# A hybrid decoder layer on one core: a new stage order, whole first transfers and a longer warm-up

## The chip, the cores and the metric

The kernel runs on one core of a Trainium2 chip. The metric is the device time of one execution in microseconds; the median of three runs is given. An execution was also recorded by the hardware profiler, and all rows of the trace come from it.

A core has five engines with instruction streams of their own: TensorE (PE in the rows; its weight loads, PEld, overlap its matmuls), VectorE (DVE), ScalarE (ACT), GpSimd (POOL) and SyncE (SP), which here issues all transfers between HBM and the on-chip memories. Engines wait for each other through semaphores.

## The reference

One layer of a decoder serves a prompt of 1024 tokens and a group of 8 sequences with 8 new tokens each (64 rows). With `D_MODEL = 1024`, the width is cut into attention A (384), convolution B (384) and memory attention M (256):

```python
hp = rmsnorm(x, norm_pre)
qa, ka, va, ga, ab, bb, gb, qm, gm = split(hp @ w_in)     # 25 blocks of 128 columns
oa = dilated_mix(rope(qa), rows, rope(ka), va)   # windows (128,1),(512,4),(2048,16), causal, 6 heads
u  = ab * sigmoid(bb)                            # GLU
ob = conformer_tail(depthwise_causal(u, w_dw))   # 31 taps, LayerNorm, swish, w_pw2
mk, mv = rmsnorm(mem_prompt) @ w_mem_kv          # 256 memory tokens, 4 heads
om = mem_attend(qm, mk, mv)
y  = x + rmsnorm(concat(oa * silu(ga), ob * silu(gb), om * silu(gm)) @ w_out, norm_post)
```

The sample group does the same with its caches: 2048 cached keys and values for A, a convolution state for B, and cached memory keys and values for M. Outputs are `y` for both groups, the new keys, values and convolution states, and both window caches shifted by the 8 new rows, which is a copy from HBM to HBM of some 50 MB in 32 transfers.

## The kernel before

**One recorded program.** The kernel does not call the engines as it goes. A class `Plan` records every operation with the buffers that it reads and writes; `schedule` then simulates the five engines with a cost model of its own, and from this comes, while the kernel is built, one fixed order of instructions for each engine. `issue` (L441, the line of nearly all rows of the trace) emits them in that order. On an engine, the ready operation of the lowest `level` goes first, and among those the one recorded first. So a place in the program is a priority, and a waiting operation is overtaken by later ones that are ready. Ten is the ordinary level; the convolution's taps are at 20, as filler on VectorE, and the 32 cache copies at 60, issued only when the modelled DMA is free. On the chip the order is fixed: an instruction that waits holds up everything behind it on its engine.

**Where the order comes from.** `ORDER` lists the stages in the order in which they are recorded: `kk`, `qq`, `vv` with a number are the projections of keys, queries and values of head pair 0 to 2, `at` the prompt's attention of that pair, `cb` a block of the convolution (its projections and then its taps), `mp` and `mk` the memory tokens' norm and projection, `kn` the sample group's new keys, `qm` the memory queries, `ma` and `ms` memory attention of the prompt and of the samples, `ga`, `gb` and `gm` gate blocks, `ct` the convolution's tail (LayerNorm and `w_pw2`), `sm` the samples' masks, `sk` and `sv` scores on the sample caches' keys and the sums over their values, `wo` the loading of the output weights, and `ot` output tiles of 128 rows, each with 24 matmuls for each half of its columns.

**Tiles and buffers.** Tokens lie along the free axis: `xT` comes as 8 tiles of 128 features by 1088 tokens. A value of 32 bits is multiplied as a high and a low part (`whi`, `wlo` for weights; pairs of `gen` tiles for x), with three matmuls in place of one. A projection block is 8 x 3 matmuls over token ranges of 512, 256 and 320 columns, 72 in all. Buffers are slots with a tag, taken when an operation that needs one is scheduled, and given back when its last user is done: `raw` (2 slots) for weights as loaded, `whi` and `wlo` (2 each) for their parts, `gen` (33) for most tiles of 128 x 1088, `tab` (2) for tables, `sm` for small columns, `mm`, `S` and `tp` for PSUM banks. A load can thus be issued only when the model sees its slot free. The sample caches come as tiles of 512 KB: `kneA` and `kneB` for keys, `vneA` and `vneB` for values; their sums are many matmuls of 32 output columns (`mm<-gen,pt`).

**The start.** `WARM` matmuls on a zero tile run on TensorE while the first transfers are under way. The first x tile and the first weights are each loaded in two pieces. Each x tile is split by `norm_split`, on ScalarE (high part) and VectorE (low part). RMSNorm's row scales need x a second time with tokens along the partitions: nine `xn` tiles, squared by ScalarE with a running sum (`squares_of`), then turned by transposes on TensorE (`rstd_of`, tile `sm` to `tp`) into a row `rstd` in a `tab` slot, with which queries and keys are scaled.

**Masks and tables.** The prompt's mask is the second `tab` tile. The samples' masks `smA` (128 x 1024) and `smB` (128 x 320) are in `gen` slots. The post-norm weights `gpost` (128 x 1024) take a `tab` slot at `wo`.

Of the kernel before, what the change touches and what calls it, by code (L numbers as in the profile page):

```python
# [21 lines left out]
KB = 8  # L22
SEQ = 1024
NS = 64
T = SEQ + NS
WARM = 12
CH = ((0, 512), (512, 768), (768, 1088))
# [93 lines left out]
class Plan:  # L121
# [148 lines left out]
    def schedule(self):  # L270
# [13 lines left out]
        port = {"V": 0.0, "G": 0.0}  # L284
        events, order, dma_free = [], [], 0.0
        table, setup, pe_end, warm = None, None, -1e9, 0
# [22 lines left out]
        now = 0  # L309
        while events:  # L310
            now = events[0][0]
# [13 lines left out]
            for e, q in queues.items():  # L325
# [4 lines left out]
                while q:  # L330
# [8 lines left out]
                    early = False  # L339
# [36 lines left out]
                if o.calls:  # L376
                    c = on(o, e)
# [6 lines left out]
                cost = o.cost  # L384
# [5 lines left out]
                if e == "PE":  # L390
                    if now - pe_end > self.COLD:
                        warm = now + 4500
                    if now < warm:
                        cost *= 2
                    if o.setup != setup:
                        cost += 95
                    setup = o.setup
                    pe_end = now + cost
# [57 lines left out]
BLOCKS += [("gb", _i) for _i in range(3)] + [("ga", _i) for _i in range(3)] + [("gm", 0), ("gm", 1)]  # L456
ORDER = "kk0 vv1 qq0 cb1 vv0 qq1 at0 kk1 at1 kk2 cb0 vv2 qq2 at2 ga0 mp cb2 qm1 kn mk qm0 ma1 ga1 ma0 ms1 ct sm ga2 gm1 sk0 sk1 gm0 sv0 gb0 gb1 gb2 wo ot2 sk2 ms0 sv1 sv2 ot4 ot0 ot7 ot8 ot1 ot3 ot5 ot6"
NAMES = dict(kk="qk", qq="qk", vv="v", at="attn", cb="conv", ct="convtail", mp="memkv", mk="memkv", kn="knew", ma="memattn",
# [6 lines left out]
def hybrid_kernel(ctx: ExitStack, tc: tile.TileContext, a: dict):  # L465
# [144 lines left out]
    for k in range(KB):  # L610
        x = t_("gen", [128, T])
        hi, lo = (t_("gen", [128, T], F32R, loose=True) for _ in range(2))
        cuts = [slice(0, 512), slice(512, T)] if k == 0 else [slice(0, T)]
        if k == 0:
            w = t_("raw", [128, KB, 128])
            first[BLOCKS[0]] = w
            SP.dma_start(w[:, early[0], :], a["w_in"][INDEX[BLOCKS[0]]][:, early[0], :])
        for c in cuts:
            SP.dma_start(x[:, c], a["xT"][k][:, c])
        if k == 0:  # L620
            SP.dma_start(w[:, early[1], :], a["w_in"][INDEX[BLOCKS[0]]][:, early[1], :])
        if k == 3:
# [666 lines left out]
    for n_, part in enumerate(parts):  # L1289
# [33 lines left out]
        elif kind == "sm":  # L1323
            smA, smB = t_("gen", [128, 1024]), t_("gen", [128, 320])
            SP.dma_start(smA, a["smA"])
# [131 lines left out]
```

## Time and profile before

| | before |
|---|---|
| runs, us | 600.92, 602.62, 603.91 |
| median of the runs, us | 602.62 |
| profiled execution, us | 600.98 |
| its span, first to last instruction, us | 599.2 |
| mean granted clock of TensorE, share of full speed | 0.989 |
| TensorE busy, us | 578.3 (97%) |
| VectorE busy, us | 441.3 (74%) |
| ScalarE busy, us | 298.2 (50%) |
| GpSimd busy, us | 124.1 (21%) |
| moved by DMA, MB | 134.96 |

The span is what the rows of the trace add up to; the execution's own time has a little around it. A clock of 1.00 in a stretch means 2.4 GHz throughout, 0.50 would be 1.2 GHz throughout. In a row of a timeline, the number in brackets is the idle time of the engine ahead of that row, and behind the arrow stands the engine, and the tile, whose work ended it. Names such as `gen` are tags, without the number of the slot.

### The profile page before, as it was taken

How to read it: one execution, taken by the hardware profiler on the slowest of the kernel's cores; microseconds unless marked ns; L12 is line 12 of the kernel's file. 1: busy time of each engine (PE TensorE's matmuls, PEld its weight loads, DVE VectorE, ACT ScalarE, POOL GpSimd, SP SyncE). 2: the span in 40 equal slices, each digit the busy share in tenths (PEclk: the TensorE clock that was granted, in tenths of full speed). 3: DMA queues.
4: the chain of work that ended last, by engine and by line, in shares of the span. 5: the costliest groups of instructions: out<-in, count | busy, mean ns of one | idle time of the engine just before them, and what ended most of it. 6: DMA issues, size and time to landing. Idle time of an engine off the chain costs nothing.

```text
span 599.2 us, 11301 instructions
## 1 busy us (share of the span) xinstructions
PE 578.3 (97%) x4466; PEld 482.5 (81%) x4466; DVE 441.3 (74%) x829; ACT 298.2 (50%) x644; POOL 124.1 (21%) x101
## 2 busy tenths in 40 slices
PE   6999999999999999999899999999999899999995
PEld 3889998778789998789898898887778667777885
DVE  4629999989993999999999999982544744226333
ACT  5676423596751138861667596761525434223221
POOL 0006644132401461011042303540000000000000
PEclk9999999999999999999999999999999799999999
DMA  8997291999996556896656032109869789781321
GB/s 300 321 379 250 76 230 51 356 333 366 309 332 249 162 145 207 332 346 193 230 201 212 34 108 73 36 4 330 310 223 379 286 323 394 284 308 73 93 101 70
DMA packets 38500, 134.96 MB, mean 225 GB/s; under 512 B 11248, under 2 KB 17904, under 8 KB 37424
## 3 DMA queue, kind: packets, MB, share of 16 engines
q1 hardware_dynamic: 38448, 134.25, 64.4%
q8 instruction: 35, 0.57, 0.4%
q14 instruction: 17, 0.14, 0.1%
HBM read 124.31 MB, written 58.87 MB: 306 GB/s over the span
## 4 chain that ended last, share of the span: by engine, by line
PE 71%; DMA 9%; DVE 8%; ACT 8%; SPq 2%; issue 2%; DVEq 0%; ACTq 0%
PE mm L441 59%; PE S L441 8%; DVE gen L441 6%; PE tp L441 5%; ACT gen L441 4%; DMA gen<-in_vneA 3%; DMA gen<-in_xn 2%; DMA gen<-in_xT 2%; SPq L441 2%; ACT e L441 2%; DMA gen<-in_kneB 1%; DMA out_cvs<-uc 1%; ACT whi L441 1%; DVE ck L441 1%; DVE e L441 1%
## 5 line engine op out<-in xcount | busy, mean ns | idle before, releaser
L441 PE MATMUL mm<-gen,whi 128*128 128x512 f32 (+3 forms) x1488 | 382.4, 343 | 4.7 <-ACT gen L441 3.7
L441 PEld LDWEIGHTS mm<-gen,whi 128*128 128x128 f32 (+1 forms) x1488 | 256.0, 189 | 38.9 <-issue 5.2
L441 PE MATMUL mm<-gen,wlo 128*128 128x512 f32 (+2 forms) x728 | 247.2, 340 | 0.0
L441 PEld LDWEIGHTS mm<-gen,wlo 128*128 128x128 f32 x728 | 137.6, 189 | 14.9 <-issue 2.8
L441 DVE SCALAR_TENSOR_TENSOR gen<-gen,cst,gen 128x1024 f32<-128x1024 f32 (+3 forms) x107 | 137.3, 1286 | 3.2 <-ACT gen L441 2.4
L441 ACT ACTIVATE whi<-raw 128x1024 fp32r<-128x1024 f32 (+1 forms) x29 | 30.5, 1052 | 58.4 <-PE mm L441 51.4
L441 ACT ACTIVATE gen<-gen 64x256 fp32r<-64x256 f32 (+6 forms) x87 | 47.2, 549 | 23.2 <-POOL gen L441 11.8
L441 ACT ACT_TABLE_LOAD x34 | 43.6, 1283 | 7.7 <-DVE sm L441 4.0
L441 ACT ACTIVATE e<-e,sm 128x320 f32<-128x320 f32 (+8 forms) x57 | 33.7, 592 | 18.3 <-DVE sm L441 17.9
L441 PE MATMUL S<-gen,gen 128*128 128x256 f32 (+7 forms) x448 | 40.5, 297 | 1.6 <-ACT gen L441 1.4
L441 PE MATMUL tp<-ident,e 128*128 128x128 f32 (+1 forms) x239 | 40.0, 278 | 0.9 <-ACT gen L441 0.5
L441 DVE TENSOR_TENSOR ck<-mm,tab 128x512 f32<-128x512 f32 (+2 forms) x48 | 25.1, 529 | 19.4 <-PE mm L441 17.9
L441 POOL TENSOR_TENSOR wlo<-raw,whi 128x1024 fp32r<-128x1024 f32 x10 | 27.3, 2734 | 57.5 <-ACT whi L441 57.5
L441 POOL TENSOR_TENSOR gen<-gen,ck 128x256 f32<-128x256 f32 (+3 forms) x17 | 16.6, 985 | 107.9 <-ACT ck L441 92.0
L441 POOL TENSOR_TENSOR pr<-uc,cst 128x496 f32<-128x496 f32 x12 | 22.1, 1838 | 72.1 <-DVE gen L441 49.9
L441 DVE TENSOR_TENSOR gen<-gen,gen 64x256 fp32r<-64x256 f32 (+4 forms) x46 | 33.6, 739 | 3.5 <-PE mm L441 1.5
L441 DVE CAST whi<-gen 128x128 fp32r<-128x128 f32 (+1 forms) x23 | 4.5, 224 | 42.7 <-PE mm L441 42.7
L441 ACT ACTIVATE e<-mm 128x512 f32<-128x512 f32 (+2 forms) x20 | 11.4, 572 | 48.6 <-PE mm L441 48.6
L441 PEld LDWEIGHTS S<-gen,gen 64*32 64x32 f32 (+1 forms) x448 | 27.6, 135 | 7.7 <-issue 2.9
L441 PEld LDWEIGHTS tp<-ident,e 128*128 128x128 f32 (+1 forms) x239 | 27.1, 137 | 8.3 <-issue 3.0
L441 DVE TENSOR_TENSOR wlo<-raw,whi 128x1024 fp32r<-128x1024 f32 (+2 forms) x20 | 25.4, 1268 | 3.0 <-ACT whi L441 2.9
L441 ACT ACTIVATE ck<-ck 128x512 f32<-128x512 f32 (+2 forms) x33 | 16.2, 502 | 21.7 <-DVE ck L441 21.6
(127 smaller groups left out, 691.6 us busy)
## 6 DMA issues: line engine op xcount, KB each, us to landing
out_wk_s<-in_kc SPq DMA_DIRECT2D x16, 1530.0 KB
out_wv_s<-in_vc SPq DMA_DIRECT2D x16, 1530.0 KB
raw<-in_w_in SPq DMA_DIRECT2D x24, 512.0 KB
gen<-in_kneA SPq DMA_DIRECT2D x24, 512.0 KB
gen<-in_vneA SPq DMA_DIRECT2D x24, 512.0 KB
gen<-in_xn SPq DMA_DIRECT2D x8, 512.0 KB
raw<-in_w_out SPq DMA_DIRECT2D x8, 512.0 KB
raw<-in_xn SPq DMA_DIRECT2D x8, 512.0 KB
```

What stands on the lines that cost most here:

```text
L441: getattr(o.real, o.method)(*[real(x) for x in o.args], **{k: real(v) for k, v in o.kw.items()})
```

## The change

Six things are edited. `WARM` rises from 12 to 18. The first x tile and the first weights are each loaded in one transfer; the weights' splitting into parts stays in two cuts (`early`). In the planner, the modelled DMA is free from 2000 ns on and not from 0, a matmul after one of another tile shape costs 105 ns and not 95, and one of the same shape behind a gap costs 80 ns more than before. `ORDER` is a new list. And `smB` moves from a `gen` slot to a `tab` slot.

```diff
-WARM = 12
+WARM = 18
...
-        events, order, dma_free = [], [], 0.0
+        events, order, dma_free = [], [], 2000.0
...
                     if o.setup != setup:
-                        cost += 95
+                        cost += 105
+                    elif now > pe_end + 1:
+                        cost += 80
                     setup = o.setup
...
-ORDER = "kk0 vv1 qq0 cb1 vv0 qq1 at0 kk1 at1 kk2 cb0 vv2 qq2 at2 ga0 mp cb2 qm1 kn mk qm0 ma1 ga1 ma0 ms1 ct sm ga2 gm1 sk0 sk1 gm0 sv0 gb0 gb1 gb2 wo ot2 sk2 ms0 sv1 sv2 ot4 ot0 ot7 ot8 ot1 ot3 ot5 ot6"
+ORDER = "kk0 vv0 qq0 vv1 cb1 qq1 at0 kk1 at1 kk2 cb0 vv2 qq2 at2 ga0 mp cb2 kn qm1 ga1 mk qm0 ga2 ma1 ma0 ms1 ct sm sk0 gm1 sk1 gm0 gb1 gb2 sv0 gb0 wo ot1 ot2 ms0 sv1 sk2 ot6 ot0 ot3 ot4 sv2 ot7 ot8 ot5"
...
         cuts = [slice(0, 512), slice(512, T)] if k == 0 else [slice(0, T)]
+        SP.dma_start(x, a["xT"][k])
         if k == 0:
-            w = t_("raw", [128, KB, 128])
-            first[BLOCKS[0]] = w
-            SP.dma_start(w[:, early[0], :], a["w_in"][INDEX[BLOCKS[0]]][:, early[0], :])
-        for c in cuts:
-            SP.dma_start(x[:, c], a["xT"][k][:, c])
-        if k == 0:
-            SP.dma_start(w[:, early[1], :], a["w_in"][INDEX[BLOCKS[0]]][:, early[1], :])
+            first[BLOCKS[0]] = load_w(BLOCKS[0])
...
-            smA, smB = t_("gen", [128, 1024]), t_("gen", [128, 320])
+            smA, smB = t_("gen", [128, 1024]), t_("tab", [128, 320])
```

What the planner makes of it shows in the order of each engine's instructions; three places are shown. The two numbers behind a tag in a name are counts, which shift with the program; the tag ahead of them is what to read. L441 of before is L443 of the changed kernel.

At the start of SyncE's order, its first loads before (`raw` is a weight tile, `gen<-in_xT` an x tile, the last number its width):

```order
L441 DMA raw_7_116<-in_w_in 128x256
L441 DMA gen_9_119<-in_xT 128x512
L441 DMA gen_9_119<-in_xT 128x576
L441 DMA raw_7_116<-in_w_in 128x768
L441 DMA gen_15_126<-in_xT 128x1088
L441 DMA gen_17_129<-in_xT 128x1088
```

And now:

```order
L443 DMA gen_7_116<-in_xT 128x1088
L443 DMA raw_9_119<-in_w_in 128x1024
L443 DMA gen_11_122<-in_xT 128x1088
L443 DMA gen_13_125<-in_xT 128x1088
L443 DMA gen_15_128<-in_xT 128x1088
```

Two issues fewer stand ahead of the second x tile. The third load of `w_in`, which stood ahead of all `xn` tiles, now stands behind the second of them.

On SyncE, the loads of the values of the first sample pair, among loads of output weights, before (a part of the twelve):

```order
L441 DMA gen_4094_5058<-in_vneA 128x1024
L441 DMA gen_4105_5071<-in_vneA 128x1024
L441 DMA gen_4108_5075<-in_vneA 128x1024
L441 DMA raw_4111_5079<-in_w_out 128x1024
L441 DMA gen_4123_5094<-in_vneA 128x1024
L441 DMA gen_4129_5102<-in_vneB 128x1024
L441 DMA gen_4142_5118<-in_vneB 128x1024
L441 DMA gen_4145_5122<-in_vneA 128x1024
L441 DMA raw_4148_5126<-in_w_out 128x1024
L441 DMA gen_4160_5140<-in_vneA 128x1024
L441 DMA gen_4165_5148<-in_vneA 128x1024
L441 DMA gen_4183_5170<-in_vneA 128x1024
```

And now:

```order
L443 DMA gen_4068_5027<-in_vneA 128x1024
L443 DMA raw_4079_5042<-in_w_out 128x1024
L443 DMA gen_4139_5115<-in_vneA 128x1024
L443 DMA raw_4149_5127<-in_w_out 128x1024
L443 DMA gen_4156_5136<-in_vneB 128x1024
L443 DMA gen_4167_5149<-in_vneB 128x1024
L443 DMA raw_4173_5156<-in_w_out 128x1024
L443 DMA gen_4177_5161<-in_vneA 128x1024
L443 DMA gen_4190_5177<-in_vneA 128x1024
L443 DMA raw_4196_5184<-in_w_out 128x1024
L443 DMA gen_4200_5189<-in_vneA 128x1024
L443 DMA gen_4203_5193<-in_vneA 128x1024
```

Two more `vneA` loads stand ahead of the rows shown of now. These first three go into slots that the keys leave; from `gen_4139` to `gen_4203` the burst holds ten transfers.

On TensorE, the memory tokens' projection (`mm` 128x256, its low weights `wlo`), before; the three matmuls on `qs` are the transposes of the new keys and the two on `sm` those of the memory's row scales:

```order
L441 MATMUL mm_2608_3252<-gen_133_292,whi_2451_3077 128x320
L441 MATMUL mm_2608_3252<-gen_124_282,wlo_2465_3094 128x320
L441 MATMUL mm_2642_3289<-ident_166,qs_607 64x128 x3
L441 MATMUL tp_2645_3293<-ident_166,sm_2313_2918 128x128 x2
L441 MATMUL mm_2647_3296<-gen_2350_2962,whi_2543_3177 128x256
L441 MATMUL mm_2647_3296<-gen_2366_2983,whi_2543_3177 128x256
L441 MATMUL mm_2647_3296<-gen_2350_2962,wlo_2559_3196 128x256
```

And now, at the new keys' transposes, and then at the memory's:

```order
L443 MATMUL mm_2549_3184<-ident_149,qs_611 64x128 x3
L443 MATMUL mm_2553_3189<-gen_25_143,whi_2448_3072 128x512
...
L443 MATMUL mm_2728_3385<-gen_136_295,whi_2548_3182 128x320
L443 MATMUL mm_2728_3385<-gen_128_286,wlo_2561_3200 128x320
L443 MATMUL tp_2759_3420<-ident_149,sm_2362_2973 128x128 x2
L443 MATMUL mm_2761_3423<-gen_2404_3023,whi_2656_3305 128x256
L443 MATMUL mm_2761_3423<-gen_2423_3045,whi_2656_3305 128x256
L443 MATMUL mm_2761_3423<-gen_2404_3023,wlo_2678_3330 128x256
```

The 144 matmuls of `qm1` and `ga1` have moved in between the two; `ga2` too now stands ahead of both blocks of the prompt's memory attention, of which one had `ga1` ahead of the other, and `gm1` alone is left to mix with them. In the same way the values of the last pair (`sv2`) have moved behind four output tiles, 106 of whose matmuls stand between the last pair's keys and them, and the first block of the convolution (`cb1`) stands behind one more value projection. Over the whole order TensorE changes tile shape between matmuls 130 times, where it was 138 times.

## Rows read from the trace of the kernel before

**Rows 1.** Section 1 of the page: busy us (share of the span) and instructions.

```profile
PE 578.3 (97%) x4466; PEld 482.5 (81%) x4466; DVE 441.3 (74%) x829; ACT 298.2 (50%) x644; POOL 124.1 (21%) x101
```

**Rows 2.** Stretches: length; busy PE, PEld, DVE, ACT, POOL; granted clock; DMA share; GB/s.

```profile
10.00:20.00 10.00, 8.14 (x36) 7.00 (x37) 9.09 (x8) 8.80 (x8) 0.00 (x0) 0.83 1.02 350
...
290.00:300.00 10.00, 8.05 (x63) 7.43 (x62) 9.30 (x18) 7.14 (x14) 0.00 (x0) 1.00 0.44 141
...
460.00:470.00 10.00, 6.94 (x131) 5.10 (x133) 8.31 (x24) 6.82 (x21) 0.94 (x3) 0.84 0.98 383
...
sum 599.20, PE 578.33 PEld 482.54 DVE 441.29 ACT 298.24 POOL 124.07; mean PE 9.64 PEld 8.04 DVE 7.35 ACT 4.97 POOL 2.07
```

**Rows 3.** TensorE in order of time: begin, us, what, [idle before, what ended it].

```profile
0.89 5.24 PE L441 MATMUL mm<-zero 128*128 128x512 bf16 x12 [0.89 <-POOL zero L441]
...
11.24 0.77 PE L441 MATMUL mm<-gen,whi 128*128 128x512 f32 x3 [2.87 <-ACT gen L441]
```

**Rows 4.** ScalarE and TensorE in order of time before the row scales.

```profile
36.21 1.06 ACT L441 ACTIVATE gen<-gen 128x1024 f32<-128x1024 f32 x1 [1.46 <-DMA gen<-in_xn]
...
40.34 1.09 PE L441 MATMUL tp<-ident,sm 128*128 128x128 f32 x8 [0.77 <-DVE sm L441]
```

**Rows 5.** TensorE in order of time at the first pair's values.

```profile
461.70 2.39 PE L441 MATMUL mm<-gen,pt 128*32 128x128 f32 x80 [0.35 <-DVE ck L441]
...
466.00 0.41 PE L441 MATMUL mm<-gen,pt 128*32 128x128 f32 x2 [1.22 <-DMA gen<-in_vneA]
467.27 0.64 PE L441 MATMUL mm<-gen,pt 128*32 128x128 f32 x2 [0.86 <-DMA gen<-in_vneA]
468.53 4.47 PE L441 MATMUL mm<-gen,pt 128*32 128x128 f32 x74 [0.63 <-DMA gen<-in_vneA]
```

**Rows 6.** SyncE's issues in order of time for these values.

```profile
448.12 3.30 SPq L441 DMA_DIRECT2D gen<-in_vneA  x3
...
455.91 2.83 SPq L441 DMA_DIRECT2D gen<-in_vneA  x3
```

**Rows 7.** SyncE's issues in order of time at the start.

```profile
1.65 0.91 SPq L441 DMA_DIRECT2D gen<-in_xT  x2
...
3.07 1.49 SPq L441 DMA_DIRECT2D gen<-in_xT  x3
```

**Rows 8.** Stretches of 2 us at the start.

```profile
4.00:6.00 2.00, 2.00 (x7) 0.77 (x4) 0.88 (x2) 0.82 (x2) 0.00 (x0) 1.00 0.92 287
...
8.00:10.00 2.00, 0.38 (x3) 0.12 (x1) 0.47 (x1) 0.85 (x2) 0.00 (x0) 1.00 1.01 400
```

**Rows 9.** TensorE in order of time around a change of tile shape.

```profile
442.20 0.31 PE L441 MATMUL mm<-gen,wlo 128*128 128x320 f32 x1
442.35 0.31 PE L441 MATMUL mm<-gen,whi 128*128 128x320 f32 x1
442.59 1.92 PE L441 MATMUL S<-gen,sq 128*32 128x512 f32 x16
```

**Rows 10.** TensorE in order of time at the memory projection's second half.

```profile
292.77 0.39 PE L441 MATMUL mm<-whi,gen 128*128 128x256 f32 x1 [0.26 <-DVE gen L441]
293.90 0.39 PE L441 MATMUL mm<-wlo,gen 128*128 128x256 f32 x1 [0.75 <-DVE wlo L441]
```

**Rows 11.** The chain that ended last: start, us, what.

```profile
51.39 31.32 PE mm L441 x186
```

**Rows 12.** TensorE in order of time at the last pair's values.

```profile
531.04 0.63 PE L441 MATMUL mm<-gen,pt 128*32 128x128 f32 x12 [0.81 <-DMA gen<-in_vneB]
...
538.70 2.37 PE L441 MATMUL mm<-gen,pt 128*32 128x128 f32 x74 [0.20 <-DMA gen<-in_vneA]
```

**Rows 13.** ScalarE's groups between 313 and 363 us, and one stretch of 5 us.

```profile
L441 ACT ACTIVATE e<-S,sm 128x256 f32<-128x256 f32 x28 | 13.0, 474 | 3.6 <-DVE sm L441 3.6
...
348.00:353.00 5.00, 5.00 (x51) 4.66 (x51) 4.76 (x11) 4.98 (x18) 0.00 (x0) 1.00 0.01 3
```

**Rows 14.** A stretch of 20 us in the middle.

```profile
180.00:200.00 20.00, 20.00 (x120) 18.04 (x119) 10.63 (x13) 2.48 (x3) 4.59 (x4) 1.00 0.66 208
```

## The prediction

> **What bounds the kernel now.** The first section of the page says where to look: TensorE is busy for 578.3 us of a 599.2 us span [rows 1]. What can be won at all are the 21 us in which it is idle, and the time in which its clock is at the lower level. The table of stretches says where these are [rows 2]. TensorE is busy for 9.64 us in the mean of 60 stretches of 10 us. The exceptions are the start (8.14 us in 10 to 20 us, at a granted clock of 0.83), the memory tokens' projection (8.05 us in 290 to 300 us), and the values of the first sample pair (6.94 us in 460 to 470 us, clock 0.84). The end, some 6 us after the last projection, is not touched by the change.
>
> Next the timelines of these places. At the start the warm-up runs from 0.89 us for 5.24 us, and TensorE then works as x tiles come; the second tile lets it go on at 11.24 us after 2.87 us of idling [rows 3], and the clock falls for part of the stretch after that. None of this reaches the end of the stage. At 40.34 us TensorE waits again, 0.77 us, for the row scales of RMSNorm, and they hang on the xn tiles: ScalarE squares the last whole one at 36.21 us, having waited 1.46 us for its transfer [rows 4]. The start is bound by that chain of transfers.
>
> At 461.70 us TensorE runs the first 80 small matmuls of the values in 2.39 us, then stops three times (1.22, 0.86 and 0.63 us) for `vneA` tiles, and the 74 matmuls from 468.53 us take 4.47 us, since the clock has fallen [rows 5]. SyncE's timeline shows the loads: the first three issued from 448.12 us, the last three from 455.91 us [rows 6]; at 383 GB/s (460 to 470 us, [rows 2]) a 512 KB tile takes 1.37 us. DMA bandwidth ends that wait.
>
> **The change, part by part.** The profiled execution took 600.98 us: 599.2 us of span and 1.8 us around it. The sum is made against that; the median of the three runs shown, 602.62 us, lies 1.64 us above it, and I add that at the end.
>
> *One transfer for the first x tile and one for the first weights, six more warm-up matmuls.* Two DMA issues of 0.4 to 0.5 us go [rows 7]; the bytes stay. The lower bound is 0, since the xn chain could be limited by its bytes alone; the upper one is the slow beginning: 287 GB/s between 4 and 6 us against 400 GB/s between 8 and 10 us [rows 8]. If whole tiles kept 400 GB/s from 4 to 8 us, 4 x 113 = 450 KB would be ahead, 1.1 us. SyncE has all of the first four x tiles issued by 4.56 us (3.07 and 1.49 us, [rows 7]), so the issues are not what is slow, and I take the lower part, **-0.3 us**. Six warm-up matmuls cost 6 x 5.24 / 12 = 2.6 us at the lower clock, half that at the higher one. They lie in the time in which weights and x tiles are on their way (TensorE's 2.87 us idle before 11.24 us), so cost 0. Without that cover they would cost 1.3 to 2.6 us. They may save the fall of the clock behind 11 us, worth 0.17 x 10 = 1.7 us of TensorE time, but what is late next is the scale transposes: TensorE arrives there earlier and waits longer. So 0 for that as well.
>
> [...]
>
> *Fewer changes of the array's shape.* Counted over the whole order, TensorE's stream changes between matmuls of different tile shape 130 times, 138 before. A 320-column matmul follows another after 0.15 us (442.20 to 442.35 us), and one with a shape change after 0.24 us (442.35 to 442.59 us) [rows 9]: 8 x 0.09 = **-0.7 us**. If the waits hide it, 0.
>
> *The memory projection.* At 292.77 and 293.90 us TensorE waits 0.26 us for a VectorE tile and 0.75 us for the low part of weights on a busy VectorE [rows 10]. In the new order 144 projection matmuls (`qm1` and `ga1`) stand between the new keys' transposes and this block; they give VectorE 144 x 0.168 = 24 us (31.32 us for 186 matmuls in the chain, [rows 11]) for the same splits: **-1.0 us**. If VectorE is late anyway, 0.
>
> *Values of the first pair.* Two of the ten value tiles that had to wait for slots freed by the last gate block now go into slots that the keys free earlier, so the late burst is ten transfers instead of twelve (w_out tiles included). Ten take 10 x 1.37 = 13.7 us and some 1.5 us until the first data; the order leaves 13.6 us of TensorE work between the first freed slot and the last tile's use. That is 1.6 us late. Twelve transfers from 448.12 to 468.53 us took 1.7 us each with their backlog; at that pace the same burst is 3.4 us late. Part of the lateness passes under packs that can run, as it did before, about 1 us of it. So an idle time of 0.6 to 2.4 us; I take 1.4 against 2.71 now, that is -1.3 us. The clock: the idling of 1.01 us at 292 to 294 us left it at 1.00 for that stretch [rows 2, 10], and 2.71 us took it down. 1.4 is nearer to the first, so I let it stay up. The price of a fall is 74 matmuls of 60 ns (4.47 us / 74) instead of 30 ns (2.39 us / 80): 2.2 us, 2.5 us with the packs after. Together **-3.8 us**; bounds -0.3 and -5.2.
>
> *Values of the last pair, later in the order.* TensorE waits 0.81 us at 531.04 us and 0.20 us at 538.70 us for such tiles [rows 12]. In the new order 106 output matmuls stand between the last keys' transposes and these values, more than 106 x 0.168 = 17 us of work for their transfers: **-1.0 us**. Were that cover gone, the wait would be as now.
>
> *The mask in the table buffer.* It takes the slot that the prompt's mask leaves, and the post-norm weights go to the other when the last gate has read the row scales; they are read first by an output tile, behind 24 matmuls per column half. 0, and at most one 1.4 us transfer if late.
>
> *Memory attention with less beside it.* Now `ga1` and `ga2` run ahead, so both attention blocks have only `gm1` to fill between. Their exponentials: 28 took ScalarE 13.0 us [rows 13], so the 32 of both blocks take 15 us; with the reads of their sums, the copies from PSUM and the table loads I estimate 25 to 30 us of ScalarE. The order gives about 25 us of TensorE work from the first transposes to the convolution's tail, and a few exponentials are done before it. Bounds 0 (all overlaps) and +5 (30 against 25). Between 348 and 353 us ScalarE was busy for 4.98 of 5 us and TensorE for all 5 [rows 13], so full is not yet late, and I take **+1.5 us**.
>
> Sum: -0.3 - 0.7 - 1.0 - 3.8 - 1.0 + 1.5 = -5.3 us, 595.7 us as an execution like the profiled one, and with 1.64 us **597.3 us** as the median.
>
> **Rivals.** (a) *The clock falls all the same*, at the values, or at the row scales, where TensorE may now idle about 3 us in place of 0.77 us. Price 2.5 us at the first place and 1.7 us at the second: 599.0 to 599.8 us, and 601.5 us with both. For it speaks that 2.87 us at the start and 2.71 us at the values both brought the clock down; against it that each place should be milder or hidden. The Trainium skill ("TensorE: Matmul & The Clock Gate", "HAM oscillation") says that idle gaps between bursts send the array back to half clock; by that rule this rival holds at both places if the gaps are as long as I fear, and the rows on the two falls agree.
>
> (b) *ScalarE becomes the bound in memory attention*: +5 instead of +1.5, 600.8 us.
>
> (c) *VectorE is late with the convolution's taps*; this one ends slower. The first convolution's projection now stands behind one more value projection, 72 x 0.168 = 12 us later on TensorE, and the taps, which fill VectorE, start that much later. VectorE has a hole to take them: 10.63 us busy in 180 to 200 us, 9.4 us free [rows 14], and work of the later gates no longer stands ahead of the last tap. If nothing of this absorbed the shift, the tail would wait 12 us: 609.3 us. It decides against the kernel when less than 3.7 us of the 12 is absorbed (605.6 us). The free 9.4 us speak against it.
>
> (d) *The start gains its upper bound*: 596.5 us. (e) *The waits only move*: what the new order takes from one place it gives back at another, 602.6 us.
>
> **How the numbers follow.** Forecast 0.42, (a) 0.22, (b) 0.13, (c) 0.10, (d) 0.07, (e) 0.06. A change of 0.5%, 3.0 us, is about what the runs can tell from none, since they spread by that (600.92 to 603.91 us). Faster (under 599.6 us) are the forecast nearly whole, (d) and half of (a): 0.60. Same are the other half of (a), most of (b), and (e): 0.27. Slower is (c) with the worst of (b): 0.13. The low end takes the best bounds of values (-1.4), start (-0.8) and attention (-1.5) together: 593.6, and 593 with rounding. The high end takes in (a), (b) and both together short of (c): 597.3 + 2.5 + 3.5 = 603.3, so 603.5 us. The forecast's own range is 595 to 599.5 us.
>
> **What would show it.** In the new profile TensorE starts real work at some 7 to 10 us without a fall of the clock before 20 us, and still waits for the row scales near 40 us (38.5 us or less would be (d)). The stretch of the memory projection shows 9 us busy or more of 10. The values of the first pair show gaps under 2 us together and a clock of 1.00. The last pair has no DMA wait. Wrong would be: ScalarE named as what ends TensorE's waits in memory attention with more than 3 us, VectorE's taps named at the tail's first matmul, or a clock below 1.00 behind 30 us.

## The result and the profile after

The changed kernel takes 608.52 us in the median of four runs (607.80 to 610.51); the kernel before took 601.77 us beside it. The ratio is 1.0121, with a 95% interval of 1.0081 to 1.0160: slower by 1.2%, where 597.3 us and a gain were forecast. The profiled execution took 610.51 us, with a span of 608.7 us.

The first section of the page of the changed kernel (busy us, share, instructions) answers to [rows 1]:

```profile
PE 581.8 (96%) x4472; PEld 483.5 (79%) x4472; DVE 440.9 (72%) x835; ACT 306.9 (50%) x651; POOL 112.2 (18%) x93
```

TensorE is busy for 3.5 us more, of which 1.5 us are the longer warm-up (6.74 against 5.24 us), and the span has grown by 9.5 us. So most of the loss is idle time. The stretches of 10 us (columns as in [rows 2]) say where:

```profile
10.00:20.00 10.00, 9.40 (x53) 8.40 (x54) 9.75 (x8) 7.61 (x7) 0.00 (x0) 1.00 1.09 335
...
100.00:110.00 10.00, 4.67 (x19) 3.75 (x19) 10.00 (x26) 3.78 (x10) 5.41 (x4) 0.77 1.04 286
110.00:120.00 10.00, 10.00 (x107) 7.03 (x106) 7.78 (x16) 4.54 (x13) 2.66 (x2) 0.89 1.04 358
...
470.00:480.00 10.00, 6.66 (x111) 4.61 (x100) 6.26 (x14) 5.45 (x16) 2.30 (x3) 0.70 0.92 363
```

The start is better than in [rows 2], busy for 9.40 of 10 us at a clock of 1.00. The stretch of the first pair's values, now from 470 to 480 us, is no better: TensorE is busy for 6.66 us of it (6.94 us before), and with the stretch behind it the time at half clock is the same (clock 0.70 and then 0.96; 0.84 and then 0.82 before). What is new stands at 100 to 120 us: TensorE was busy for 10.00 and 9.71 us there before, and is now for 4.67 us of the first 10, at a clock of 0.77 and then 0.89. The first of these stretches in the kernel before:

```profile
100.00:110.00 10.00, 10.00 (x94) 7.81 (x93) 9.96 (x23) 6.60 (x17) 0.32 (x1) 1.00 0.78 239
```

The timeline of the changed kernel names the two waits (start, us, what, idle before and what ended it):

```profile
101.48 0.70 PE L443 MATMUL mm<-gen,whi 128*128 128x512 f32 x2 [1.23 <-DVE ck L443]
...
107.20 0.79 PE L443 MATMUL S<-gen,gen 128*128 128x256 f32 x2 [4.11 <-DVE sm L443]
...
112.19 0.34 PE L443 MATMUL S<-gen,gen 64*32 64x64 f32 x16
```

5.34 us of idling, both ended by VectorE, at the beginning of the first attention block. So the next view is VectorE's timeline before that:

```profile
88.48 1.77 DVE L443 TENSOR_SCALAR gen<-gen,cst 128x1024 f32<-128x1024 f32 x1
95.91 1.23 DVE L443 TENSOR_TENSOR wlo<-raw,whi 128x1024 fp32r<-128x1024 f32 x1 [5.67 <-ACT whi L443]
97.05 1.28 DVE L443 SCALAR_TENSOR_TENSOR gen<-gen,cst,gen 128x1024 f32<-128x1024 f32 x1
...
106.86 0.28 DVE L443 CUSTOM_DVE_ANT_0 e<-S,tab 128x128 f32<-128x128 f32 x1
```

VectorE is busy without a gap from 95.91 us to the instruction that frees TensorE at 106.86 us. It is late because it stood still for 5.67 us before 95.91 us, ahead of `wlo`, the low part of a block of weights. Behind that in its order stand taps of the convolution (the `SCALAR_TENSOR_TENSOR` rows), which come between TensorE and what it needs. `wlo` waits for `whi`, and ScalarE's timeline says what that waited for:

```profile
94.82 1.06 ACT L443 ACTIVATE whi<-raw 128x1024 fp32r<-128x1024 f32 x1 [17.77 <-DMA raw<-in_w_in]
```

The weights came late. SyncE's timeline has the reason:

```profile
54.62 0.33 SPq L443 DMA_DIRECT2D raw<-in_w_in  x1
...
55.90 32.89 SPq L443 DMA_DIRECT2D gen<-gen  x48
...
89.51 1.71 SPq L443 DMA_DIRECT2D raw<-in_w_in  x2
```

The load of these weights is issued at 89.51 us, behind 48 small transfers that take SyncE 32.89 us, 0.685 us each. They are the second half of `v_block`: 24 copies of 16 KB, from one `gen` tile to another, lay the values of a head pair out anew. It is not their bytes that take this time, since the DMA engines are nearly idle while the copies are issued (share 0.11, 25 GB/s):

```profile
70.00:80.00 10.00, 10.00 (x63) 9.18 (x62) 5.84 (x10) 3.30 (x6) 3.06 (x4) 1.00 0.11 25
```

With `vv0` and `vv1` now almost side by side in the list, the copies of both come in one run. The kernel before had them in two, with the weight loads between:

```profile
56.34 16.27 SPq L441 DMA_DIRECT2D gen<-gen  x24
...
75.05 0.33 SPq L441 DMA_DIRECT2D raw<-in_w_in  x1
...
78.80 0.33 SPq L441 DMA_DIRECT2D raw<-in_w_in  x1
83.81 18.94 SPq L441 DMA_DIRECT2D gen<-gen  x24
```

That is a wait in SyncE's queue which the prediction didn't see. The half clock behind it adds to the idling.

The places that the prediction did name, in TensorE's timeline of the changed kernel:

```profile
27.18 1.25 PE L443 MATMUL mm<-gen,whi 128*128 128x512 f32 x6 [2.22 <-ACT whi L443]
...
39.48 1.09 PE L443 MATMUL tp<-ident,sm 128*128 128x128 f32 x8 [0.86 <-DVE sm L443]
...
309.91 0.39 PE L443 MATMUL mm<-gen,wlo 128*128 128x256 f32 x1 [0.64 <-DVE wlo L443]
...
471.93 0.41 PE L443 MATMUL mm<-gen,pt 128*32 128x128 f32 x2 [0.68 <-DMA gen<-in_vneA]
474.41 0.64 PE L443 MATMUL mm<-gen,pt 128*32 128x128 f32 x2 [2.07 <-DMA gen<-in_vneA]
475.64 4.48 PE L443 MATMUL mm<-gen,pt 128*32 128x128 f32 x74 [0.60 <-DMA gen<-in_vneA]
...
517.57 2.37 PE L443 MATMUL mm<-gen,pt 128*32 128x128 f32 x74 [0.84 <-DMA gen<-in_vneA]
...
533.44 0.63 PE L443 MATMUL S<-gen,sq 128*32 128x256 f32 x4 [0.17 <-DMA gen<-in_kneB]
534.69 1.06 PE L443 MATMUL S<-gen,sq 128*32 128x256 f32 x12 [0.62 <-DMA gen<-in_kneB]
```

The row scales ([rows 4]) begin 0.86 us earlier; ahead of them TensorE now also waits 2.22 us for the third block of weights, whose load stands behind two `xn` tiles. In this execution that does no harm, since TensorE still has to wait for the row scales behind it. The memory projection ([rows 10]) still waits for `wlo`, 0.64 us. The first pair's values ([rows 5]) wait 0.68, 2.07 and 0.60 us, and the 74 matmuls behind them still run at half clock. The last pair's values ([rows 12]) wait no more, but the second pair's do (0.84 us at 517.57 us), and the last pair's keys (0.17 and 0.62 us).

### The profile page after: what moved, and what is told of

Read it like the earlier page. It is cut to its first block, busy times and chain, and to the rows that moved or that the text cites. A ratio compares the mean times of both kernels' runs of the same rounds, so it can differ in the third digit from the quotient of the medians.

```text
span 608.7 us, 11363 instructions
## 1 busy us (share of the span) xinstructions
PE 581.8 (96%) x4472; PEld 483.5 (79%) x4472; DVE 440.9 (72%) x835; ACT 306.9 (50%) x651; POOL 112.2 (18%) x93
## 4 chain that ended last, share of the span: by engine, by line
PE 64%; DVE 13%; DMA 10%; ACT 7%; issue 3%; SPq 2%; POOL 0%; DVEq 0%; ACTq 0%; POOLq 0%
PE mm L443 52%; DVE gen L443 8%; PE S L443 7%; PE tp L443 5%; ACT gen L443 4%; DMA gen<-in_vneA 3%; DMA gen<-in_xn 3%; SPq L443 2%; DVE ck L443 2%; ACT e L443 1%; DMA gen<-in_xT 1%; DVE wlo L443 1%; DMA gen<-in_kneB 1%; DMA out_cvs<-uc 1%; DVE sm L443 1%
## 5 line engine op out<-in xcount | busy, mean ns | idle before, releaser
L443 PE MATMUL mm<-gen,whi 128*128 128x512 f32 (+3 forms) x1488 | 382.0, 343 | 4.4 <-ACT whi L443 2.4
L443 PEld LDWEIGHTS mm<-gen,whi 128*128 128x128 f32 (+1 forms) x1488 | 256.0, 188 | 37.4 <-ACT whi L443 4.5
L443 PE MATMUL mm<-gen,wlo 128*128 128x512 f32 (+2 forms) x728 | 248.2, 342 | 0.6 <-DVE wlo L443 0.6
L443 PEld LDWEIGHTS mm<-gen,wlo 128*128 128x128 f32 x728 | 137.2, 189 | 15.9 <-issue 2.6
L443 DVE SCALAR_TENSOR_TENSOR gen<-gen,cst,gen 128x1024 f32<-128x1024 f32 (+3 forms) x107 | 136.8, 1285 | 6.6 <-ACT gen L443 5.5
L443 ACT ACTIVATE whi<-raw 128x1024 fp32r<-128x1024 f32 (+2 forms) x30 | 30.7, 1029 | 65.1 <-PE mm L443 38.4
L443 ACT ACTIVATE gen<-gen 64x256 fp32r<-64x256 f32 (+3 forms) x84 | 45.6, 551 | 22.0 <-POOL gen L443 10.2
L443 PE MATMUL S<-gen,gen 128*128 128x256 f32 (+7 forms) x448 | 41.2, 300 | 5.1 <-DVE sm L443 4.3
L443 ACT ACTIVATE e<-e,sm 128x320 f32<-128x320 f32 (+8 forms) x57 | 33.7, 592 | 22.3 <-DVE sm L443 22.1
L443 PE MATMUL tp<-ident,e 128*128 128x128 f32 (+1 forms) x239 | 40.3, 280 | 2.1 <-ACT e L443 0.9
L443 POOL TENSOR_TENSOR gen<-gen,ck 128x256 f32<-128x256 f32 (+3 forms) x18 | 21.4, 1192 | 94.4 <-ACT ck L443 75.2
L443 PEld LDWEIGHTS S<-gen,gen 64*32 64x32 f32 (+1 forms) x448 | 28.2, 137 | 12.2 <-DVE sm L443 5.1
L443 PEld LDWEIGHTS tp<-ident,e 128*128 128x128 f32 (+1 forms) x239 | 27.0, 138 | 11.6 <-ACT e L443 4.9
L443 POOL TENSOR_TENSOR pr<-uc,cst 128x496 f32<-128x496 f32 x12 | 22.4, 1864 | 72.3 <-DVE gen L443 41.9
L443 DVE TENSOR_TENSOR ck<-mm,tab 128x512 f32<-128x512 f32 (+2 forms) x48 | 25.1, 528 | 14.6 <-PE mm L443 13.0
L443 ACT ACTIVATE pt<-tp 128x512 f32<-128x512 f32 (+3 forms) x48 | 25.0, 532 | 17.9 <-PE tp L443 14.3
L443 DVE TENSOR_TENSOR wlo<-raw,whi 128x1024 fp32r<-128x1024 f32 (+2 forms) x23 | 26.8, 1170 | 9.3 <-ACT whi L443 9.2
L443 ACT ACTIVATE ck<-ck 128x512 f32<-128x512 f32 (+2 forms) x33 | 16.4, 504 | 31.9 <-DVE ck L443 31.7
L443 DVE TENSOR_TENSOR gen<-gen,gen 64x256 fp32r<-64x256 f32 (+4 forms) x49 | 31.3, 646 | 1.0
L443 DVE CAST whi<-gen 128x128 fp32r<-128x128 f32 (+1 forms) x26 | 4.9, 216 | 35.5 <-PE mm L443 35.4
L443 POOL TENSOR_TENSOR wlo<-raw,whi 128x1024 fp32r<-128x1024 f32 x7 | 18.7, 2666 | 60.3 <-ACT whi L443 60.3
```

The costliest lines, as they stand in the source:

```text
L443: getattr(o.real, o.method)(*[real(x) for x in o.args], **{k: real(v) for k, v in o.kw.items()})
```

## The experiments

Twelve kernels were run. Theory 1 is that of SyncE's queue. The rivals were the later start of the convolution's taps (the prediction's own rival (c)), and the start, warm-up or planner constants.

**Four kernels by the planner.** The first has the changed kernel with the stage list of before:

```diff
-ORDER = "kk0 vv0 qq0 vv1 cb1 qq1 at0 ... ms1 ct sm sk0 gm1 sk1 gm0 gb1 gb2 sv0 gb0 wo ot1 ot2 ms0 sv1 sk2 ..."
+ORDER = "kk0 vv1 qq0 cb1 vv0 qq1 at0 ... ms1 ct sm ga2 gm1 sk0 sk1 gm0 sv0 gb0 gb1 gb2 wo ot2 sk2 ms0 sv1 ..."
```

> The changed kernel with the stage list of before; start, warm-up, planner costs and mask slot stay new. Theory 1 (SyncE's queue: the 48 small transfers of two value projections stand in one run of 32.89 us, the weights of the next projection are issued behind them at 89.51 us, and VectorE and then TensorE wait, 5.34 us and a fall of the clock): the run is cut in two again, so the loss of some 7 us goes; the other new order is gone as well, and I expect 600 to 603 us, no idle stretch above 1 us and no fall of the clock between 60 and 130 us. Rival 2 (VectorE is late with the taps since the convolution starts later): the same, 600 to 603. Rival 3 (the longer warm-up, the whole first transfers or the planner's new costs bring the loss): 607 to 609 us.

Measured: 615.92 us, ratio 1.0244 (1.0221 to 1.0268). Near 100 us there is no stall. But it is 14 us slower than the kernel before, which has the same list, and none of the theories said so. The old list together with the other edits gives another order for all engines. TensorE's timeline of this kernel shows one of the new waits, at the first output tile, whose weights are loaded late:

```profile
481.02 0.80 PE L443 MATMUL mm<-gen,whi 128*128 128x512 f32 x1 [4.18 <-ACT gen L443]
```

The second kernel is the one before, with the new list alone.

> The kernel before with the new stage list alone. Theory 1 and rival 2: the run of 48 transfers is there, so a stall of 4 to 6 us near 100 us and 606 to 610 us in all. Rival 3: about 602 us, no such stall.

Measured: 622.07 us, ratio 1.0346 (1.0313 to 1.0380), more than any theory had. The stall is there, with waits of 1.09 and 4.10 us at 102.07 and 107.79 us, as theory 1 and the taps have it; the start and the constants, which are old here, are not its cause. The rest of its loss is again spread over later stages (4.28 us in one wait on VectorE at 529 us). So of these two only the stretch near 100 us tells something about the change; their total times tell that, as this planner orders them, the new list and the other edits are each worse alone than together.

The third lets weight loads overtake the small copies:

```diff
+        P.level = 12
         for b in range(6):
             for r in range(4):
                 SP.dma_start(vf[i][32 * (b % 4):32 * (b % 4) + 32, r + 4 * (b // 4), :], vt[i][32 * r:32 * r + 32, b, :])
+        P.level = 10
```

> The changed kernel with the small value transfers at level 12, so that weight loads overtake them in SyncE's order; the stage list and the place of the convolution stay as changed. Theory 1: the weights come in time, the stall near 100 us goes, 600 to 603 us. Rival 2 (the taps come later on VectorE because the convolution stands behind one more value projection): the convolution is where it was, so 607 to 609 us and the stall stays. Rival 3: 607 to 609 us.

Measured: 606.84 us, ratio 1.0087 (1.0061 to 1.0113). By its time alone this looked like a miss for theory 1. The stretches say otherwise:

```profile
100.00:110.00 10.00, 10.00 (x96) 7.79 (x95) 10.00 (x24) 6.87 (x17) 3.11 (x3) 1.00 1.07 198
...
390.00:400.00 10.00, 8.69 (x47) 6.80 (x46) 9.58 (x28) 9.56 (x16) 3.21 (x4) 0.88 0.00 0
```

TensorE is busy for 10 of 10 us at a clock of 1.00 from 100 to 110 us; the stall is gone, with the convolution where the change put it. What was won was lost again in later stages, whose order the planner drew up anew as well (1.3 us of idling and a clock of 0.88 in the convolution's tail). In this execution the clock also fell at the start, to 0.88 from 30 to 40 us.

The fourth swaps two neighbours in the list:

```diff
-ORDER = "kk0 vv0 qq0 vv1 cb1 qq1 ..."
+ORDER = "kk0 vv0 qq0 cb1 vv1 qq1 ..."
```

> The changed kernel with one swap in the stage list: the first convolution block ahead of the second value projection again, so that the small transfers come in two runs of 24. Theory 1 and rival 2: the stall near 100 us goes, 600 to 603 us. Rival 3: 607 to 609 us.

Measured: 600.72 us, ratio 0.9985 (0.9966 to 1.0005). The loss is gone. This agrees with theory 1 and with the taps alike, since the swap moves both.

**Three kernels in which only SyncE's order changes.** To leave the planner out, the next ones edit the finished order just before it is emitted. The rows of all other engines stay as in the changed kernel, one by one.

```diff
     def issue(self):
+        q = self.order
+        runs = [n for n, o in enumerate(q) if o.method == "dma_start" and o.bytes == 16384]
+        late = [o for o in q[runs[47]:] if o.method == "dma_start" and o.bytes == 524288 and o.bufs[0].tag == "raw"][:2]
+        for o in late:
+            at = q.index(o)
+            last = max(n for n, x in enumerate(q[:at]) if any(b.slot == o.bufs[0].slot for b in x.bufs))
+            q.insert(last + 1, q.pop(at))
```

> The changed kernel with the orders of TensorE, VectorE, ScalarE and GpSimd untouched, instruction by instruction; in SyncE's order alone two weight loads move from behind the 48 small transfers to behind the 15th and the 40th, as early as their slots are free. Theory 1 (the weights queue behind the small transfers): the first load is issued at some 67 us in place of 89.51 us, TensorE's two waits of 1.23 and 4.11 us near 100 us go and the clock stays at 1.00, 600 to 602 us. Rival 2 (VectorE's order itself, with three taps among the steps of the keys' rotation, makes TensorE wait): the waits stay, 606 to 609 us.

Measured: 600.79 us, ratio 0.9970 (0.9949 to 0.9991). SyncE's timeline has the loads where the edit put them:

```profile
66.52 0.34 SPq L450 DMA_DIRECT2D raw<-in_w_in  x1
66.91 16.13 SPq L450 DMA_DIRECT2D gen<-gen  x25
83.13 0.53 SPq L450 DMA_DIRECT2D raw<-in_w_in  x1
```

In TensorE's timeline the two waits are gone; two rows to measure by, the row scales and a pack of 16 score matmuls behind the stall:

```profile
39.08 1.09 PE L450 MATMUL tp<-ident,sm 128*128 128x128 f32 x8 [0.24 <-DVE sm L450]
...
104.07 0.34 PE L450 MATMUL S<-gen,gen 64*32 64x64 f32 x16
```

In the changed kernel the same rows begin at 39.48 and 112.19 us. Between them the stall has cost 72.71 - 64.99 = 7.72 us: 5.34 us of idling, and the rest, 2.4 us, is put down to the half clock behind it. Against the changed kernel's 1.0121 the ratio fell by 0.015, some 9 us. That shows theory 1. The taps have the same place on VectorE as in the changed kernel, and TensorE has no wait for VectorE near 100 us, so nothing there is left for them to explain.

Each of the two loads alone, with `[:1]` and `[1:2]` in the place of `[:2]`:

> The changed kernel with only the first of the two weight loads moved, from behind the 48 small transfers to behind the 15th; every other engine's order as changed. Theory 1: this is the load on which VectorE waits 5.67 us, so this alone brings back nearly all, 600 to 602.5 us. Rival (the second load, whose weights are needed later, is late as well and holds as much): 604 us or more.

> The changed kernel with only the second of the two weight loads moved, to behind the 40th small transfer. Theory 1: the first load is issued behind all 48 as before, the stall near 100 us stays, 606 to 609 us (up to 1.4 us less, since one transfer fewer runs beside the late one). Rival: 604 us or less.

Measured: with the first load moved 601.36 us, ratio 0.9995 (0.9972 to 1.0018); with the second 607.43 us, ratio 1.0113 (1.0069 to 1.0157). So it is the first load that matters; with the second alone the ratio stays at the changed kernel's 1.0121 within the noise. In the kernel with the second moved, TensorE's two waits (1.49 and 4.09 us) and the one of VectorE stand as in the changed kernel; VectorE's row:

```profile
96.69 1.23 DVE L450 TENSOR_TENSOR wlo<-raw,whi 128x1024 fp32r<-128x1024 f32 x1 [5.93 <-ACT whi L450]
```

**The warm-up.** The kernel of the swap, with six warm-up matmuls fewer and no other edit:

```diff
     def issue(self):
+        warm = [o for o in self.order if o.eng == "PE"][12:18]
+        self.order = [o for o in self.order if o not in warm]
```

> The kernel of the swap (first convolution ahead of the second value projection) with all orders untouched, but only 12 of the 18 warm-up matmuls issued. As predicted (the six lie under the transfers and what follows waits for the row scales): within 0.5 us of the swap's 600.7 us, though the clock may fall before 20 us. Rival (the clock's fall at the start is paid in full, or the six are): 1.3 to 2.6 us either way.

Measured: 601.46 us, ratio 0.9992 (0.9972 to 1.0013), no difference that these runs can tell from the swap's 0.9985. TensorE then idles 1.93 us before its first real matmul, its clock is 0.91 and 0.92 in the first two stretches of 10 us, and it waits longer for the row scales, which begin no later:

```profile
7.45 0.91 PE L445 MATMUL mm<-gen,whi 128*128 128x512 f32 x3 [1.93 <-ACT whi L445]
...
38.81 1.09 PE L445 MATMUL tp<-ident,sm 128*128 128x128 f32 x8 [1.55 <-DVE sm L445]
```

**The values of the first pair.** Why did they wait as long as before? Two kernels with the swap move loads in SyncE's order: first the post-norm weights and one load of output weights, which are issued behind the last value tiles, then also the loads of output weights that are issued among these tiles (each as far back as its first reader allows).

```diff
+        g = next(o for o in loads if o.bufs[0].tag == "tab")
+        w = loads[loads.index(g) + 1]
...
+        q.insert(read - 1, q.pop(b))
+        q.insert(far, q.pop(a))
...
+        for o in loads[:loads.index(g)][-3:]:
+            q.insert(min(read - 1, last), q.pop(at))
```

> The kernel of the swap, SyncE's order alone edited: the post-norm weights and the load of output weights behind them, 1 MB issued after the last value tile of the first pair, are issued some 5 to 10 us later. Theory V1 (transfers under way share the bandwidth, so that later ones slow the last value tiles): the waits of 2.05 and 0.83 us shrink by 1 to 2 us and 1 to 3 us are gained. Theory V2 (transfers are served in the order of issue): the waits stay, no gain.

> As the run before it, and two more loads of output weights moved behind value tiles of the first pair's burst. V1 and V2 both: the last value tiles land 1.4 us earlier for each of the loads that is now behind them, the three waits (0.27, 2.05, 0.83 us) shrink to less than 1 us together, the clock stays at 1.00 and 2 to 5 us are gained, 596 to 599 us, unless ScalarE, which waits for these weights in its order, holds TensorE up in their place (then 600 us or more). Theory V3 (not the bytes but the moment at which slots come free sets the last tile): no gain.

Measured: 605.09 us, ratio 1.0046 (1.0024 to 1.0068), and 610.40 us, ratio 1.0143 (1.0116 to 1.0171). Both are slower than the swap. TensorE's timeline of the first:

```profile
466.23 0.64 PE L454 MATMUL mm<-gen,pt 128*32 128x128 f32 x2 [2.29 <-DMA gen<-in_vneA]
467.47 4.48 PE L454 MATMUL mm<-gen,pt 128*32 128x128 f32 x74 [0.60 <-DMA gen<-in_vneA]
...
474.83 0.44 PE L454 MATMUL mm<-ident,sq 128*128 128x128 f32 x2 [1.42 <-ACT sq L454]
```

The waits for value tiles (2.29 and 0.60 us) hardly shrink against the swap's 0.27, 2.05 and 0.83 us. The last two value tiles are also issued 1.7 us later here (459.83 against 458.12 us), so this kernel doesn't decide whether later transfers slow earlier ones. A new wait of 1.42 us for ScalarE has come in. TensorE's timeline of the second:

```profile
463.86 4.50 PE L460 MATMUL mm<-gen,pt 128*32 128x128 f32 x80 [4.42 <-DVE ck L460]
...
468.78 2.39 PE L460 MATMUL mm<-gen,pt 128*32 128x128 f32 x80
...
478.18 0.69 PE L460 MATMUL mm<-ident,sq 128*128 128x128 f32 x2 [5.76 <-ACT sq L460]
```

And ScalarE's, the first of three such rows:

```profile
460.89 1.06 ACT L460 ACTIVATE gen<-raw 128x1024 fp32r<-128x1024 f32 x1 [9.46 <-DMA raw<-in_w_out]
```

ScalarE stands 9.46, 3.74 and 5.12 us for output weights, with work behind it that TensorE needs, and TensorE waits 4.42 and 5.76 us for that. No wait for a value tile is left, but TensorE also comes to the last of them later, so this doesn't show how much earlier they landed. What it shows is that the loads are wanted at the same time, and that one order or the other pays. Neither kernel settles whether the bytes ahead or the slots set the last tile, but the second leans to the slots. With two of the three loads of output weights gone from among them, its seven value tiles are still issued over 8.59 us (448.86 to 457.45 us; 9.15 us in the swap's kernel, 449.86 to 459.01 us). And the waits of SyncE itself from 448.9 to 457.6 us, six of 10.8 us in total with the one ahead of the first of these tiles, all end with matmuls of TensorE, which give slots back:

```profile
SPq L460 <- PE mm L460: 10.8, 6, 5.5
```

The stretches of 2 us of the changed kernel (clock, DMA share, GB/s at the end) say more:

```profile
458.00:460.00 2.00, 2.00 (x13) 1.78 (x13) 1.69 (x3) 0.86 (x1) 1.21 (x1) 1.00 0.60 221
...
464.00:466.00 2.00, 2.00 (x14) 1.82 (x13) 1.14 (x1) 0.82 (x1) 0.00 (x0) 1.00 0.89 344
466.00:468.00 2.00, 2.00 (x15) 1.79 (x13) 0.65 (x2) 0.00 (x0) 0.00 (x0) 1.00 1.02 395
...
470.00:472.00 2.00, 1.32 (x34) 0.66 (x24) 2.00 (x3) 1.91 (x9) 1.88 (x2) 1.00 1.02 418
```

The transfers come to some 400 GB/s only from 466 us on. Before that SyncE's issues are spread, from 457.65 to 466.96 us for the ten of the burst, and the DMA engines move 277 GB/s in the mean of the four stretches from 458 to 466 us (221, 258, 285 and 344).

**The clock.** Matmuls on the zero tile are put into the waits for value tiles, in the kernel with the two loads ahead (2, 8 and 3 of them) and in the kernel before (4, 3 and 3):

```diff
+        for at, count in list(zip(spots, (0, 2, 8, 3)))[::-1]:
...
+            for _ in range(count):
+                x = Op()
+                x.eng, x.real, x.method, x.args, x.kw, x.mark, x.bufs = "PE", warm.real, "matmul", (out,), warm.kw, "fill", [buf]
+                x.bytes = 0
+                q.insert(at, x)
```

> As the kernel with the two weight loads moved ahead, and 13 matmuls on the zero tile (2, 8 and 3) put on TensorE into the three waits for value tiles of the first pair, which were 0.59, 2.10 and 0.84 us; all other engines' orders are untouched. As predicted of the clock (idling brings it down, and the fall costs some 2.2 to 2.5 us behind it): the 74 matmuls behind the waits take 2.4 us and not 4.5, the clock stays at 1.00 from 460 to 480 us, and some 2 us are gained on 600.8 us: 598 to 599.5 us, below both kernels. Rival (the half clock there is hidden, because the transfers set the pace behind the waits too): within 0.5 us of 600.8 us.

> The kernel before with ten matmuls on the zero tile (4, 3 and 3) in its three waits for value tiles of the first pair (1.22, 0.86 and 0.63 us), nothing else. As predicted of the clock: the 74 matmuls behind take 2.4 us in place of 4.47 us and the kernel gains 2 to 2.5 us. Rival: no gain.

Measured: 600.22 us, ratio 0.9983 (0.9962 to 1.0004), and 601.30 us, ratio 0.9992 (0.9968 to 1.0016). The clock does what was expected; the time doesn't. The first kernel was to take 598 to 599.5 us, and its ratio is no lower than without the filler (0.9970). TensorE's timeline of the first of the two:

```profile
470.28 2.37 PE L474 MATMUL mm<-gen,pt 128*32 128x128 f32 x74
...
474.70 0.44 PE L474 MATMUL mm<-ident,sq 128*128 128x128 f32 x2 [0.81 <-ACT sq L474]
```

And of the second, the kernel before with filler:

```profile
460.40 2.39 PE L465 MATMUL mm<-gen,pt 128*32 128x128 f32 x80 [0.35 <-DVE ck L465]
...
466.59 2.37 PE L465 MATMUL mm<-gen,pt 128*32 128x128 f32 x74
...
471.01 0.44 PE L465 MATMUL mm<-ident,sq 128*128 128x128 f32 x2 [0.81 <-ACT sq L465]
```

74 matmuls take 2.37 us, where [rows 5] had 4.47 us. From the first pack of values to the transposes of the next stage (`mm<-ident,sq`) the kernel before needed 12.62 us (461.70 to 474.32 us) and needs 10.61 us with the filler; 0.81 us of it is now a wait for ScalarE. In whole times the gain doesn't show here either: 0.5 us, with an interval of 1.0 us slower to 1.9 us faster. A gain of 2 us is just outside of it. In its profile later loads of the samples take 1.0 us of the gain back: 0.67 us of a new wait for `kneB` at 491.30 us, and 1.12 us in place of 0.81 us for `vneB` at 529.39 us.

## Why the prediction was wrong

**The step that failed** is the count of what a moved stage brings with it. In rival (c) the prediction wrote that the convolution now stands behind one more value projection, "72 x 0.168 = 12 us later on TensorE". It priced the projection's matmuls and left out its 24 copies on SyncE, though they are in `v_block` and in the order of SyncE. The trace of before had all that was needed: 24 copies take 16.27 us at one place and 18.94 us at another, and the weight loads at 75.05 and 78.80 us stood between them. In a row they take 16.27 + 18.94 = 35 us, from 56.34 us on, so a load behind them is issued near 91 us, and has to come, be split and be multiplied where the kernel before had it ready. The cost is 7.72 us in the trace, and no term of the sum was about this place: the sum put it at nothing. The Trainium skill has a rule that bears on this: "DMA: Bandwidth & Descriptors", "Rules for kernel authors", says to coalesce many small transfers into one large, since under 64 KB one pays mostly overhead. The trace agrees, with 0.685 us of SyncE for each 16 KB. The same page ("Issuing engines are not separate DMA queues") calls the time to initiate a transfer usually small beside the transfer. That does not hold for these: issuing them keeps SyncE occupied for 32.89 us, while the DMA engines are at a share of 0.11.

**Rival (c)** had the right sign and the wrong mechanism. The taps are what VectorE had still to do when it could go on, but moving one load brings the time back with every tap in its place. That its 609.3 us lies next to the measured 608.52 us is chance: it is the sum of 12 us of late taps at the convolution's tail and a gain of 5.3 us elsewhere, while the kernel lost 7.7 us near 100 us and gained much less elsewhere. The start and the planner's constants are cleared of this stall by the kernel with the new list alone.

**The other terms**, for which the kernel with the two loads ahead is the changed kernel without the stall: it gains 0.3% on before (0.1 to 0.5%), about 1.8 us, where the sum had 5.3 us.

- *Start* (-0.3 us, at most -1.1): the row scales begin 0.86 us earlier in the changed kernel and 1.26 us in that one, but single executions differ by more than that. In ten profiled kernels with the same orders at the start as the changed kernel they begin between 38.47 and 40.73 us, at 39.5 us in the mean; in the three with the old start between 39.74 and 40.34 us, at 40.1 us in the mean. So the term is right in kind, some 0.6 us, and poorly known. The clock stays at 1.00 from 10 to 40 us in seven of the ten, and is 0.87 to 0.89 from 30 to 40 us in the other three, although TensorE waits about as long for the third weights before that (1.7 to 3.0 us in the seven, 1.8 to 2.7 us in the three). The six warm-ups are hidden, as the kernel without them shows.
- *Memory projection* (-1.0 us): 0.64 us of waiting for `wlo` is left of 1.01 us, in this execution; in three of the other kernels the same wait takes 2.26 to 2.28 us. The 24 us of cover didn't bring the split forward; why VectorE did it no earlier was not tried.
- *Values of the first pair* (-3.8 us): this is the second wrong step. The idle time came out at 3.35 us (3.53 us with the two loads ahead), not 1.4 us, and beyond the 2.4 us that were taken as the bound, and so the clock fell as before. The burst of ten was counted at 1.37 us a tile, the pace of [rows 2], and 1.5 us. It took 18.0 us from the issue at 457.65 us to the first use of its last tile at 475.64 us, 1.8 us a transfer, slower even than the 1.7 us that the prediction took for its upper bound. The prediction reckoned with 383 GB/s from the first transfer on; 8 us at 277 GB/s make 2.2 of the 2.8 us between 15.2 and 18.0 us (8 x 106 / 383). What spreads the issues wasn't settled; the waits of SyncE shown above lean to the slots. Rival (a) was right for this place; its price of 2.5 us measured 2.0 us locally, with the filler in the kernel before. The Trainium skill ("TensorE: Matmul & The Clock Gate", "HAM oscillation") says that idle gaps between bursts send the array back to half clock. The traces agree, with 4.48 us for the 74 matmuls behind the gaps and 2.37 us where the gaps are filled. Two numbers of the term were loose from the start. The 1.5 us until the first data had no row behind them, and no run shows them by themselves: in the trace of before a load of 384 KB issued at 301.55 us was used at 305.00 us, 3.45 us later, where its bytes take 1.0 us at 383 GB/s. And the bound of -5.2 us takes no idling at all, where the prediction's own 0.6 us makes it -4.6 us.
- *Values of the last pair* (-1.0 us): that wait is gone, but 0.84 us has moved to the second pair and 0.79 us to the last pair's keys, more than was saved. With the two loads ahead only 0.20 us is left.
- *Memory attention* (+1.5 us): 0.55 us is lost in one wait at 347.97 us, and ScalarE ended it (`pt`), but ScalarE was busy for only 4.21 us from 340 to 350 us. It is not the bound there, and rival (b) did not come.
- *Shape changes* (-0.7 us) and *the mask*: no run took them alone, so they stay open.

The planner's part in it can be read but was not tested: its `cost` gives 470 ns to each `dma_start`, large or small, and the chip took 685 ns for each of these 48, so by this cost the plan would have the weights some 48 x 0.215 = 10 us earlier than they came, and it put `wlo` ahead of the taps on VectorE.

## What to carry to other kernels

When a stage moves, list what it issues on every queue, the small copies above all, and add up the issuing engine's time: what is queued behind the longest run is the next thing to be late. In an order that is fixed when the kernel is built, a late load can cost more than the wait for it, since everything behind the waiting instruction stands too, on every engine down the chain: here 5.67 us on VectorE became 7.72 us on TensorE, part of it at half clock. And an order that a list scheduler draws up shouldn't be taken apart by running the planner again on half of the edits; editing the finished order of one queue changes one thing, and settled in one kernel what four planned ones had left open.

## What the runs showed of the hardware

- The time of an issue on SyncE did not follow the bytes: 0.685 us for each of 48 copies of 16 KB in a row (0.68 and 0.79 us in the two runs of before), against 0.33 us for a single load of weights of 512 KB, and 0.53 us for one right behind such copies.
- The same orders do not give the same start: the clock from 30 to 40 us was 1.00 in seven of ten profiled kernels and 0.87 to 0.89 in three, and the row scales began between 38.47 and 40.73 us.
- Work of no use in a wait keeps the clock of TensorE up, 2.37 us in place of 4.47 us for 74 matmuls, and the whole kernel gained too little of it to measure.
